# One weight pool kept open from the gate stage to branch A, and two staging buffers in place of three for the key and value stage

## The chip, the core and the metric

The kernel runs on one core of one Trainium2 chip. The core has five engines that run side by side, each through its own list of instructions in a fixed order: TensorE (PE in the profile) multiplies matrices, VectorE (DVE) and GpSimd (POOL) work on elements, ScalarE (ACT) applies functions and copies, and SyncE (SP) issues transfers. ACT issues transfers too, from the same list as its arithmetic, so a transfer or an operation that waits holds up everything behind it on ACT. All transfers run on 16 shared DMA engines. On-chip memory (SBUF) is given below as an address in KB of one partition; every tile takes all 128 partitions. PSUM has eight banks, and a bank can take the next product only when the last one has been read out of it.

The metric is the device time of one launch in microseconds, the median of several runs.

## The reference

One block of a transformer-like trunk over 1024 tokens of width 1024, all in float32:

```python
h = rmsnorm(x, ln1_g) * (1 + sc1) + sh1
q, k, v, cb, cc, cx, ga, gb = split(h @ w_in)          # eight column blocks of 1024
q, k = rmsnorm per head of q, k                        # 16 heads of 64
y_a = stick_breaking_attention(q, k, v)
y_b = cb * causal_dwconv(cc * cx, conv_w)
x = x + g1 * ((sigmoid(ga) * (y_a @ w_branch_a) + sigmoid(gb) * (y_b @ w_branch_b)) @ w_out)
h = rmsnorm(x, ln2_g) * (1 + sc2) + sh2
x = x + g2 * ((silu(h @ w_gate) * (h @ w_up)) @ w_down)
```

The six modulation vectors (sh1, sc1, g1, ...) come from a product of silu(c) with `ada_w`.

## The kernel before, in words

Every large product is done in three matmuls: each float32 operand is split into a high part (`hi`, written by ACT) and a rest (`lo`, written by DVE or POOL), and hi x hi, hi x lo and lo x hi are added up in PSUM. A weight therefore passes through a staging tile: SP loads it into `raw` (4 KB), ACT copies the high part out of `raw` into `whi`, DVE subtracts to make `wlo`, and then `raw` is free for the next load. How many `raw` tiles there are decides how far SP's loads run ahead of the splits.

The stages stand in this order:

1. **Start** (lines 141 to 330): load x transposed, compute the norm and the modulation, make `hh` and `hl` (the two parts of h, in four `big` tiles) one 128-row block k after the other, and begin the first product group, half of v, as the blocks come. Its weights come through `load_wq` and `split_wq`, from the pool `wpa` with three `raw` tiles and six tiles each of `whi` and `wlo`.
2. **Key and value stage** (lines 333 to 423): three column groups, `cc` = 0 (half of v), 1 and 2 (k), each over eight token tiles i. A tile's product takes 24 matmuls into one PSUM bank. In group 0 seven of the eight products are already in PSUM when this loop starts and only lack their last block, so seven `finish_v` follow each other closely. `finish_v` (line 391) copies the product out of PSUM with ACT (line 394), subtracts with DVE (line 395), which frees the bank, and stores the 4 KB tile `vs` to the DRAM scratch `d_v` from ACT's queue (line 396). `finish_k` (line 369) squares, normalizes and transposes a tile of k, makes its two parts in a tile `khl` (lines 385 and 386) and stores them to `d_k` with two transfers from ACT's queue (line 388). `vs` and `khl` share one tag with three buffers. A buffer can be written again when its store has landed. Beside this, `factors` (line 342) forms sums of h for the Strassen products, with POOL, ACT (line 358) and DVE, in the pool `phm` on the right side of SBUF.
3. **Gate stage** (lines 425 to 644): 20 rounds, each the product of h with two blocks of 128 columns, by Strassen's scheme with seven smaller products each (`half_prod`, lines 122 to 124). Weights come through `g_raw` and `g_split` (lines 428 and 435) from the pool `gw`, with two `raw` and four `whi` and `wlo` tiles of half the size. The first two products of the first two gates (`first_two`) stand ahead of the loop. For the loop, SP reloads parts of the factors: two transfers of 1 MB into `hh` and `hl` (line 581) and one of 2 MB into `ft6` (line 579). The loop begins with ACT's copy of the first product out of PSUM (line 617) and the split of the sums `ws` of the weights.
4. **Attention** (lines 653 to 887): the scores, scans and products of 16 heads, with the rest of v, the products of branch B and its projection mixed in as filler for PE. The filler's weights come through the same `g_raw` and `g_split`.
5. **Branch A's projection** (lines 908 to 939), again through `g_raw` and `g_split`; then the output projection (`w_o`), the second norm, the feed-forward products with pools of their own.

Each pool's place in SBUF is settled when it opens, on the left or the right end of what is free. `gw` is a pool named `wpg` at 167 to 191 KB during the gate stage. It opens at line 422, when `phm` has closed, on the place where `phm` was. It closes at line 645, and a pool `wpb` of the same size opens at 199 to 223 KB, where the tiles `ft5` and `ft4` were that the last gate's products read. `wpb` stays open until line 1005.

The order of each engine's instructions is settled at build time by a scheduler that knows the tiles' sizes and places and lets an instruction wait for the last user of the memory that it takes. A run of the program does not reorder anything.

Of the kernel before, what the change touches and what calls it, by code (L numbers as in the profile page):

```python
# [8 lines left out]
F32 = mybir.dt.float32  # L9
F32R = mybir.dt.float32r  # L10
# [6 lines left out]
P = 128  # L17
# [12 lines left out]
def block_kernel(tc, x, x_t, cols, ada_1, ada_2, ada_row, w_q, w_kv, w_v1, w_cg, w_a, w_b, w_o, w_g, w_u, w_d, out):  # L30
# [8 lines left out]
    def nm(s):  # L39
        uid[0] += 1  # L40
        return f"{s}_{uid[0]}"
# [1 line left out]
    def big():  # L43
        return bigp.tile([P, KT, 512], F32R, tag="big", bufs=4, name=nm("big"))

    wps = [None, 0, 0]

    def open_w(name, nraw, n):

        es = ExitStack()  # L50
        wps[:] = [es.enter_context(tc.tile_pool(name=name, bufs=1, reuse_waits="tile")), nraw, n]
        return es

    def load_w(src):

        wp, nraw, bufs = wps
        raw = wp.tile([P, 1024], F32, tag="raw", bufs=nraw, name=nm("raw"))
        nc.sync.dma_start(raw, src)
        hi = wp.tile([P, 1024], F32R, tag="whi", bufs=bufs, name=nm("whi"))
        lo = wp.tile([P, 1024], F32R, tag="wlo", bufs=bufs, name=nm("wlo"))  # L60
        nc.scalar.activation(hi, raw, AF.Copy)
        nc.vector.tensor_tensor(out=lo, in0=raw, in1=hi.bitcast(F32), op=ALU.subtract)
        return hi, lo
# [74 lines left out]

    md = ps_pj()

    sw = open_w("wpa", 3, 6)
    def in_order(i0):

        prev = {}
# [26 lines left out]
        ads.append(ad)  # L171

    def load_wq(qt):
        wp, nraw, bufs = wps
        raw = wp.tile([P, 1024], F32, tag="raw", bufs=nraw, name=nm("raw"))
        nc.sync.dma_start(raw, w_kv[0, qt])
        hi = wp.tile([P, 1024], F32R, tag="whi", bufs=bufs, name=nm("whi"))
        lo = wp.tile([P, 1024], F32R, tag="wlo", bufs=bufs, name=nm("wlo"))
        wraw.append(raw)
        wq.append((hi, lo))  # L180
# [153 lines left out]
    ap = s2.enter_context(tc.tile_pool(name="pha", bufs=1, reuse_waits="tile"))  # L334
# [34 lines left out]
    def finish_k(ps, i, ch):  # L369
        sq = ap.tile([P, 512], F32, tag="qsq", bufs=2, name=nm("qsq"))  # L370
        nc.scalar.activation(sq, ps, AF.Square)
        ss = ap.tile([P, 8], F32, tag="qss", bufs=3, name=nm("qss"))
        nc.vector.tensor_reduce(out=ss, in_=sq.rearrange("p (h d) -> p h d", d=DH), op=ALU.add, axis=AX.X)
        qn = ap.tile([P, 512], F32, tag="qn", bufs=2, name=nm("qn"))
        r = rstd_of(ss, 1.0 / DH, ap, 8)
        nc.vector.tensor_tensor(out=qn.rearrange("p (h d) -> p h d", d=DH),
                                in0=ps.rearrange("p (h d) -> p h d", d=DH),
                                in1=r.unsqueeze(2).broadcast_to([P, 8, DH]), op=ALU.mult)
        yield
        tr = ps_tr()  # L380
        for j in range(4):
            nc.tensor.transpose(tr[:, j * P:(j + 1) * P], qn[:, j * P:(j + 1) * P], ident)
        hl_ = ap.tile([P, 2, 512], F32R, tag="vs", bufs=3, name=nm("khl"))
        hi, lo = hl_[:, 0], hl_[:, 1]
        nc.scalar.activation(hi, tr, AF.Identity, scale=kgc)
        nc.vector.scalar_tensor_tensor(out=lo, in0=tr, scalar=kgc, in1=hi.bitcast(F32), op0=ALU.mult, op1=ALU.subtract)
        for e, t in ((0, hi), (1, lo)):
            nc.scalar.dma_start(d_k[e][4 * ch:4 * ch + 4, :, i * P:(i + 1) * P].rearrange("j p t -> p j t"),
                                t.rearrange("p (j t) -> p j t", j=4).bitcast(F32))

    def finish_v(ps, i, ch):
        vs = ap.tile([P, 8, P], F32R, tag="vs", bufs=3, name=nm("vs"))
        pv = ps.rearrange("p (h d) -> p h d", d=DH)
        nc.scalar.activation(vs[:, :, :DH], pv, AF.Copy)
        nc.vector.tensor_tensor(out=vs[:, :, DH:], in0=pv, in1=vs[:, :, :DH].bitcast(F32), op=ALU.subtract)
        nc.scalar.dma_start(d_v[8 * ch:8 * ch + 8, :, i, :].rearrange("h p d -> p h d"), vs.bitcast(F32))

    GR, NG, GS = 2, 2, 4
    tails = []
    for cc in range(3):  # L400
        w = wq if cc == 0 else [load_w(w_kv[cc, j]) for j in range(4)]
        for i in ((5, 6, 0, 1, 2, 3, 4, 7) if cc == 0 else range(8)):
            if cc == 0 and i < NPRE:
                ps = pss[i]
                mm_tok(ps, i, w, 7, 8)
            else:
                ps = ps_pj()
                mm_tok(ps, i, w, 0, 8)
            while len(tails) >= 2:
                next(tails.pop(0), None)  # L410
            if cc > 0:
                tails.append(finish_k(ps, i, cc - 1))
                next(tails[-1])
            else:
                finish_v(ps, i, 0)
            for _ in range(2 if cc else 0):
                next(ml, None)
            if (cc, i) == (2, 4):
                for _ in ml:
                    pass  # L420
                s2b.close()
                gws = ExitStack()
                gw = gws.enter_context(tc.tile_pool(name="wpg", bufs=1, side="right", reuse_waits="tile"))

    def g_bank():
        return ps_pj()
# [155 lines left out]
    for g, (sec, j) in enumerate(gates):  # L582
        raw, raw2 = raws
# [58 lines left out]
        for _ in range((0 if sec == 5 else 3) if g + 1 < len(gates) else 50):  # L642
            next(ml, None)
    sg_.close()
    gws.close()
    ftx.close()
    gws = ExitStack()
    gw = gws.enter_context(tc.tile_pool(name="wpb", bufs=1, side="right", reuse_waits="tile"))
    for e in range(2):
        nc.sync.dma_start((hh, hl)[e][1][:, :4].bitcast(F32), d_h[e])  # L650
    psA.close()
# [259 lines left out]
    for n in range(2):  # L911
        for k in range(KT):
            yr = fp.tile([P, 512], F32, tag="yr", bufs=2, name=nm("yr"))
            nc.sync.dma_start(yr, d_ya[n][:, k, :])
            tag, bufs = slots[n * KT + k]
# [23 lines left out]
            nc.vector.tensor_tensor(out=mlo[n][:, m, :], in0=sa, in1=mh[n][:, m, :].bitcast(F32), op=ALU.subtract)  # L939
    s3.close()  # L940
    fpool.close()
    psB.close()


# [2 lines left out]
    sw = ExitStack()  # L947
    wp = sw.enter_context(tc.tile_pool(name="wpd", bufs=1, reuse_waits="tile"))
# [49 lines left out]
    for ch in range(2):  # L998
        w = [] if ch else list(w_pre)
        for j in range(len(w) // 2, 4):  # L1000
            raw = load_raw(w_o[ch, j])
            w += [split(raw[:, c * 512:(c + 1) * 512]) for c in range(len(w) % 2, 2)]
        if ch == 1:
            swx.close()
            gws.close()
            rqs.close()
            s5 = ExitStack()
            hp = s5.enter_context(tc.tile_pool(name="phh", bufs=1, side="right", reuse_waits="tile"))

            h2t = {q: hp.tile([P, 4, 512], F32, name=f"h2b{q}") for q in ("01", "11", "t2", "00", "10")}  # L1010
            h2b = [[h2t[f"{e}{n}"] for n in range(2)] for e in range(2)]
            t2f = h2t["t2"]
        cs = slice(ch * 512, ch * 512 + 512)
        for i in range(8):
            n, t0 = i // 4, (i % 4) * P
            xi = dp.tile([P, 512], F32, tag="xr", bufs=3, name=nm("xr"))
            nc.scalar.dma_start(xi, x[i * P:(i + 1) * P, cs])
            ps = bank()
            for k in range(KT):
                nc.tensor.matmul(ps, mh[n][:, k, t0:t0 + P], w[k][0], start=(k == 0), stop=False)  # L1020
                nc.tensor.matmul(ps, mh[n][:, k, t0:t0 + P], w[k][1], start=False, stop=False)  # L1021
                nc.tensor.matmul(ps, mlo[n][:, k, t0:t0 + P], w[k][0], start=False, stop=(k == KT - 1))  # L1022
            tm = dp.tile([P, 512], F32, tag="tm", bufs=2, name=nm("tm"))
            nc.vector.tensor_tensor(out=tm, in0=ps, in1=g1b[:, cs], op=ALU.mult)
            if ch == 0:
                nc.vector.tensor_tensor(out=tm, in0=tm, in1=xi, op=ALU.add)
                nc.scalar.dma_start(d_x1[i, :, cs], tm)
                continue
            x1 = dp.tile([P, D], F32, tag="x1", bufs=2, name=nm("x1"))
            nc.scalar.dma_start(x1[:, :512], d_x1[i, :, :512])  # L1030
            nc.vector.tensor_tensor(out=x1[:, cs], in0=tm, in1=xi, op=ALU.add)
            nc.scalar.dma_start(d_x1[i, :, cs], x1[:, cs])
            ss = dp.tile([P, 1], F32, tag="ss", bufs=3, name=nm("ss"))
            xn = dp.tile([P, D], F32, tag="xn", bufs=2, name=nm("xn"))
            nc.scalar.activation(xn, x1, AF.Square, accum_out=ss)  # L1035
            r = rstd_of(ss, 1.0 / D, dp, 1)
            nc.scalar.activation(xn, x1, AF.Copy, scale=r[:, 0:1])
            if tails:
                norm2_tail(*tails.pop())
            tails.append((i, xn))  # L1040
            if i == 4:
                bh, bl = big(), big()
            if i == 5:
                for e in range(2):
                    split_big(bh[:, 4 * e:4 * e + 4], bl[:, 4 * e:4 * e + 4], h2b[e][0])
# [11 lines left out]
    for key, src in (((0, 0), w_g), ((0, 1), w_u), ((1, 0), w_g)):  # L1057
        raw = load_raw(src[key[0]])
# [291 lines left out]
```

## Time and profile before

| | |
|---|---|
| runs, us | 1946.02, 1945.4, 1941.25; median 1945.4 |
| profiled execution, us | 1945.62, of which the span from first to last instruction 1943.8 |
| PE busy in the span | 1853.6 us (95%) |
| DVE, ACT, POOL busy | 1462.3, 864.6, 673.7 us |
| mean DMA rate | 179 GB/s |
| mean granted TensorE clock | 0.986 |

The profile is one execution. A row of its timeline has the start and the duration in us, the engine (with a q where it is the issue of a transfer), the line, the operation, what it writes and reads, how many equal ones were merged into the row, and in brackets how long the engine had been idle and what ended that. A row of the waits has who waited for whom, the sum in us, how many times, and the longest. Lines named in rows are those of the listing above. Names stand without their numbers, so that all `vs` tiles are `vs`, and the matrix-product banks of the early stages are `pj`.

### The profile page before, as it was taken

How to read it: one execution, taken by the hardware profiler on the slowest of the kernel's cores; microseconds unless marked ns; L12 is line 12 of the kernel's file. 1: busy time of each engine (PE TensorE's matmuls, PEld its weight loads, DVE VectorE, ACT ScalarE, POOL GpSimd, SP SyncE). 2: the span in 40 equal slices, each digit the busy share in tenths (PEclk: the TensorE clock that was granted, in tenths of full speed). 3: DMA queues.
4: the chain of work that ended last, by engine and by line, in shares of the span. 5: the costliest groups of instructions: out<-in, count | busy, mean ns of one | idle time of the engine just before them, and what ended most of it. 6: DMA issues, size and time to landing. Idle time of an engine off the chain costs nothing.

```text
span 1943.8 us, 25154 instructions
## 1 busy us (share of the span) xinstructions
PE 1853.6 (95%) x8869; PEld 1519.5 (78%) x8869; DVE 1462.3 (75%) x1927; ACT 864.6 (44%) x1597; POOL 673.7 (35%) x475
## 2 busy tenths in 40 slices
PE   7899999998999999998999999979999999999899
PEld 4678767777888888887888788867888888878587
DVE  8865687778664799998999644499988788743854
ACT  4442343223333677776777421464444434422221
POOL 3694547978231001111000000065454444301713
PEclk8899999999999999999999999999999999999999
DMA  6465544334445756559554535323343334399566
GB/s 276 162 208 172 190 154 160 136 114 152 170 171 197 214 158 189 169 167 302 161 161 128 189 130 193 133 82 136 146 173 152 141 143 171 119 347 321 218 221 224
DMA packets 151149, 347.47 MB, mean 179 GB/s; under 512 B 15088, under 2 KB 52208, under 8 KB 149104
## 3 DMA queue, kind: packets, MB, share of 16 engines
q1 hardware_dynamic: 74000, 218.80, 34.4%
q10 hardware_dynamic: 76016, 123.40, 17.6%
q0 software_dynamic: 1008, 3.67, 0.5%
q8 instruction: 70, 1.15, 0.2%
q14 instruction: 55, 0.45, 0.1%
HBM read 235.19 MB, written 110.62 MB: 178 GB/s over the span
## 4 chain that ended last, share of the span: by engine, by line
PE 43%; DVE 10%; issue 3%; DMA 3%; ACT 2%; POOL 1%; ACTq 0%; SPq 0%; DVEq 0%; POOLq 0%
PE e L122 6%; PE e L124 6%; PE e L123 6%; PE e L1203 3%; PE e L1204 3%; PE e L1202 3%; PE pj L785 3%; PE pj L786 3%; PE pj L787 3%; DVE pt L710 2%; DVE wlo L965 2%; PE e L1020 1%; PE e L1022 1%; PE e L1021 1%; PE tr L726 1%
## 5 line engine op out<-in xcount | busy, mean ns | idle before, releaser
L710 DVE TENSOR_TENSOR_SCAN pt<-pt,dm 128x256 f32<-128x256 f32 (+7 forms) x128 | 173.9, 1363 | 5.3 <-ACT pt L705 5.1
L123 PE MATMUL e<-big,whi 128*128 128x512 f32 x352 | 138.0, 392 | 7.8 <-DVE big L127 7.8
L122 PE MATMUL e<-big,whi 128*128 128x512 f32 x352 | 137.7, 392 | 0.8 <-ACT c L1118 0.8
L124 PE MATMUL e<-big,wlo 128*128 128x512 f32 x352 | 137.5, 391 | 0.0
L1203 PE MATMUL e<-wlo,f 128*128 128x512 f32 (+1 forms) x319 | 123.1, 386 | 9.5 <-DVE wlo L965 9.5
L124 PE MATMUL pj<-big,wlo 128*128 128x512 f32 x320 | 127.0, 398 | 5.1 <-DVE wlo L127 5.1
L113 POOL TENSOR_SCALAR rs_m<-ss 128x1 f32<-128x1 f32 x8 | 2.0, 245 | 365.3 <-ACT xn L1035 365.3
L122 PE MATMUL pj<-big,whi 128*128 128x512 f32 x320 | 128.0, 400 | 0.4 <-ACT whi L438 0.4
L276 PE MATMUL pj<-whi,big 128*128 128x512 f32 x352 | 116.3, 410 | 11.6 <-ACT big L263 8.9
L123 PE MATMUL pj<-big,whi 128*128 128x512 f32 x320 | 127.1, 397 | 0.0
L705 ACT ACTIVATE pt<-z,rq 128x512 f32<-128x512 f32 (+2 forms) x192 | 112.3, 587 | 30.5 <-PE z L704 17.6
L1204 PE MATMUL e<-whi,f 128*128 128x512 f32 (+1 forms) x319 | 121.8, 382 | 0.0
L1202 PE MATMUL e<-whi,f 128*128 128x512 f32 (+1 forms) x319 | 118.5, 383 | 2.0 <-ACT fs L1142 1.4
L127 DVE TENSOR_TENSOR c<-e,c 128x512 f32<-128x512 f32 x154 | 102.8, 681 | 21.1 <-PE e L124 21.1
L829 POOL TENSOR_TENSOR ybl<-cy,ybh 128x512 fp32r<-128x512 f32 x16 | 29.0, 1810 | 255.7 <-ACT ybh L828 242.9
L438 ACT ACTIVATE whi<-raw 128x512 fp32r<-128x512 f32 x116 | 72.7, 633 | 94.4 <-PE pj L123 32.6
L706 ACT ACTIVATE sg<-z,rq 128x512 f32<-128x512 f32 (+1 forms) x192 | 112.7, 590 | 1.3 <-DVE mb L851 1.3
L127 DVE TENSOR_TENSOR c<-pj,c 128x512 f32<-128x512 f32 x140 | 93.2, 681 | 24.3 <-PE pj L124 24.1
L127 DVE TENSOR_TENSOR wlo<-ws,whi 128x512 fp32r<-128x512 f32 x80 | 73.6, 939 | 50.0 <-ACT whi L438 49.8
L730 DVE TENSOR_TENSOR atl<-tr,ath 128x512 fp32r<-128x512 f32 (+1 forms) x192 | 100.3, 544 | 10.7 <-ACT ath L729 10.3
L127 POOL TENSOR_TENSOR ws<-raw,raw 128x512 f32<-128x512 f32 x41 | 57.9, 1412 | 144.1 <-DMA raw<-w_cg 80.7
L729 ACT ACTIVATE ath<-tr 128x512 fp32r<-128x512 f32 (+1 forms) x192 | 90.4, 498 | 37.8 <-PE tr L726 12.7
(250 smaller groups left out, 5641.9 us busy)
## 6 DMA issues: line engine op xcount, KB each, us to landing
f<-d_f SPq DMA_DIRECT2D x77, 512.0 KB, 4.4
d_f<-fs ACTq DMA_DIRECT2D x70, 512.0 KB, 2.6
raw<-w_cg SPq DMA_DIRECT2D x40, 512.0 KB, 3.4
mada<-ada ACTq DMA_DIRECT2D x32, 512.0 KB, 4.2
raw<-w_g SPq DMA_DIRECT2D x24, 512.0 KB, 3.2
raw<-w_u SPq DMA_DIRECT2D x23, 512.0 KB, 3.2
d_k<-khl ACTq DMA_DIRECT2D x32, 256.0 KB, 2.2
d_q<-gt ACTq DMA_DIRECT2D x32, 256.0 KB, 2.1
```

Of the source, the lines that this page charges most:

```text
L122: nc.tensor.matmul(ps, wh[:, k, :], fh[:, k, :], start=(k == 0), stop=False)
L123: nc.tensor.matmul(ps, wh[:, k, :], fl[:, k, :], start=False, stop=False)
L124: nc.tensor.matmul(ps, wl[:, k, :], fh[:, k, :], start=False, stop=(k == 3))
L127: eng.tensor_tensor(out=out, in0=a, in1=b, op=op)
L276: nc.tensor.matmul(ps, a, b, start=(k == 0 and q == 0), stop=(k == KT - 1 and q == 2))
L705: nc.scalar.activation(pt[:, off + s0:off + s0 + m], z[:, :m], AF.Sigmoid, scale=rq[:, 1, i, h:h + 1])
L706: nc.scalar.activation(sg[:, s0:s0 + m], z[:, :m], AF.Sigmoid, scale=rq[:, 0, i, h:h + 1])
L710: nc.vector.tensor_tensor_scan(out=pt[:, rev], data0=pt[:, rev], data1=dm[:, rev], initial=0.0, op0=ALU.mult, op1=ALU.add)
L730: nc.vector.tensor_tensor(out=tl[:, :nb, c0:c0 + P], in0=src, in1=th[:, :nb, c0:c0 + P].bitcast(F32), op=ALU.subtract)
L1202: nc.tensor.matmul(o, sh, w[0][:, c], start=(j == 0), stop=False)
L1203: nc.tensor.matmul(o, sh, w[1][:, c], start=False, stop=False)
L1204: nc.tensor.matmul(o, sl, w[0][:, c], start=False, stop=(j == NJ - 1))
```

## The change

One pool `gw`, named `wpl`, with two `raw` tiles and four half-size `whi` and `wlo` tiles, opens ahead of the first weight pool at 85 to 109 KB and closes after branch A's projection. It takes the place of `wpg` and `wpb`. The start stage and the key and value stage no longer have `raw` tiles of their own: they use the two of this pool. `vs` and `khl` have two buffers in place of three. `wpa` now holds only `whi` and `wlo` and lies at 109 to 157 KB; the pools behind it on the left move up by 12 KB (start, key and value stage) or 24 KB (gate stage, attention), and the attention's pools on the right move into the 24 KB that `wpb` had. The first weights of the output projection (`wpx`) move with them by 24 KB; everything behind that lies where it was. No arithmetic and no transfer is added or removed.

```diff
-    wps = [None, 0, 0]
+    wps = [None, 0]
-    def open_w(name, nraw, n):
+    def open_w(name, n):
         es = ExitStack()
-        wps[:] = [es.enter_context(tc.tile_pool(name=name, bufs=1, reuse_waits="tile")), nraw, n]
+        wps[:] = [es.enter_context(tc.tile_pool(name=name, bufs=1, reuse_waits="tile")), n]
         return es
     def load_w(src):
-        wp, nraw, bufs = wps
-        raw = wp.tile([P, 1024], F32, tag="raw", bufs=nraw, name=nm("raw"))
+        wp, bufs = wps
+        raw = gw.tile([P, 1024], F32, tag="raw", bufs=GR, name=nm("raw"))
         nc.sync.dma_start(raw, src)
...
-    sw = open_w("wpa", 3, 6)
+    GR, NG, GS = 2, 2, 4
+    gws = ExitStack()
+    gw = gws.enter_context(tc.tile_pool(name="wpl", bufs=1, reuse_waits="tile"))
+    sw = open_w("wpa", 6)
...
     def load_wq(qt):
-        wp, nraw, bufs = wps
-        raw = wp.tile([P, 1024], F32, tag="raw", bufs=nraw, name=nm("raw"))
+        wp, bufs = wps
+        raw = gw.tile([P, 1024], F32, tag="raw", bufs=GR, name=nm("raw"))
...
-        hl_ = ap.tile([P, 2, 512], F32R, tag="vs", bufs=3, name=nm("khl"))
+        hl_ = ap.tile([P, 2, 512], F32R, tag="vs", bufs=2, name=nm("khl"))
...
-        vs = ap.tile([P, 8, P], F32R, tag="vs", bufs=3, name=nm("vs"))
+        vs = ap.tile([P, 8, P], F32R, tag="vs", bufs=2, name=nm("vs"))
...
-    GR, NG, GS = 2, 2, 4
     tails = []
...
                 s2b.close()
-                gws = ExitStack()
-                gw = gws.enter_context(tc.tile_pool(name="wpg", bufs=1, side="right", reuse_waits="tile"))
...
     sg_.close()
-    gws.close()
     ftx.close()
-    gws = ExitStack()
-    gw = gws.enter_context(tc.tile_pool(name="wpb", bufs=1, side="right", reuse_waits="tile"))
...
     fpool.close()
+    gws.close()
     psB.close()
...
             swx.close()
-            gws.close()
             rqs.close()
```

## The prediction

> **What bounds the kernel now.** I read the page's head, then the busy time by stage, then what PE waited for.
>
> ```profile
> span 1943.8 us, 25154 instructions
> PE 1853.6 (95%) x8869; PEld 1519.5 (78%) x8869; DVE 1462.3 (75%) x1927; ACT 864.6 (44%) x1597; POOL 673.7 (35%) x475
> ```
>
> ```profile
> 85.00:192.00 107.00, 104.91 (x485) 85.74 (x484) 64.17 (x77) 38.43 (x62) 77.21 (x63) 1.00 0.57 180
> 192.00:620.00 428.00, 413.51 (x1768) 325.26 (x1767) 307.96 (x370) 144.74 (x240) 247.05 (x162) 0.99 0.45 158
> 620.00:1085.00 465.00, 441.64 (x2727) 384.90 (x2726) 426.85 (x612) 338.07 (x726) 29.14 (x20) 0.99 0.63 186
> 1085.00:1132.00 47.00, 47.00 (x199) 37.84 (x199) 24.65 (x38) 14.48 (x24) 0.00 (x0) 0.97 0.57 188
> 1132.00:1300.00 168.00, 163.98 (x742) 133.13 (x741) 90.51 (x135) 63.98 (x106) 21.76 (x25) 1.00 0.41 141
> ```
>
> The columns are the stretch, its length, then busy time of PE, PEld, DVE, ACT and POOL, the granted clock, DMA share and GB/s. The stretches are key and value stage, gates, attention, branch A, output projection with second norm. PE is the bound in every one of them: it idles 2.1 of 107 us in the key and value stage and nothing in branch A. So a change of buffers can win only what PE waits at the places it touches, and loses whatever new wait reaches PE. The built order of the changed program has the same instructions on every engine (8811 PE rows of the listing, 1934 ACT, 587 SP), so nothing is priced by count, only by waits and order.
>
> **What can be won.** The moved weight tiles touch three borders. Key and value to gates:
>
> ```profile
> 206.86 0.57 PE L122 MATMUL pj<-ft,whi 128*128 128x512 f32 x1 [2.06 <-ACT whi L438]
> ```
>
> Gates to attention (PE's waits between 596 and 660):
>
> ```profile
> PE z L703 <- ACT sg L706: 1.7, 1, 1.7
> PE pj L805 <- DVE wlo L127: 0.5, 1, 0.5
> PE pj L804 <- DVE vs L810: 0.4, 1, 0.4
> ```
>
> Branch A to output projection: PE is full to 1132 and loses 4 us in the next 168, spread over the second norm, so nothing is left there. At the second border the filler's weights no longer wait for the last gate products that read `ft5` and `ft4`, and stand two places earlier in SP's queue. I count the two small waits, 0.5 + 0.4 = 0.9 us, as gone (term C, -0.9; bounds 0 and all three, -2.6; the 1.7 hangs on a sigmoid and not on a weight, so I leave it). The 2.06 at the first border is no wait for the pool that moves, as term B shows.
>
> **Term A: two buffers for `vs`, and the burst of seven.** ACT, DVE and PE around 92 to 102:
>
> ```profile
> 92.94 0.60 ACT L394 ACTIVATE vs<-pj 128x512 fp32r<-128x512 f32 x1
> 94.69 1.07 ACT L61 ACTIVATE whi<-raw 128x1024 fp32r<-128x1024 f32 x1 [0.30 <-PE pj L276]
> 97.14 1.04 ACT L61 ACTIVATE whi<-raw 128x1024 fp32r<-128x1024 f32 x1
> 98.09 0.58 ACT L394 ACTIVATE vs<-pj 128x512 fp32r<-128x512 f32 x1
> ```
>
> ```profile
> 93.81 0.68 DVE L395 TENSOR_TENSOR vs<-pj,vs 128x512 fp32r<-128x512 f32 x1
> 99.12 2.31 DVE L62 TENSOR_TENSOR wlo<-raw,whi 128x1024 fp32r<-128x1024 f32 x1
> 101.36 0.68 DVE L395 TENSOR_TENSOR vs<-pj,vs 128x512 fp32r<-128x512 f32 x1
> ```
>
> ```profile
> 102.19 0.47 PE L276 MATMUL pj<-whi,big 128*128 128x512 f32 x1 [0.74 <-DVE vs L395]
> 96.00:101.45 5.45, 5.45 (x25) 4.17 (x23) 1.00 1.01 329
> L396 ACTq DMA_DIRECT2D d_v<-vs x3: 384/422/1803, 93.3 to 94.7; - x3
> DMA to landing us min/median/max: 4.1/5.2/5.8
> ```
>
> The first two `vs` of the burst come from the transpose banks; the third, at 92.94, frees on DVE at 93.81 + 0.68 = 94.49 the bank of the first product of k, the fourth (101.36, done at 102.04) that of the second. PE runs k's first product from 96.00 to 101.45 (24 matmuls; the window counts one that overlaps its edge) and then waits 0.74 for the second bank. With two buffers the third `vs` waits until the first store has landed: issued at 93.3, plus 4.1, is 97.4. In the changed order ACT's copy stands behind both weight splits (94.69, 97.14), and DVE's subtraction behind the second L62, which ends at 101.4. So the third takes the fourth's place, 98.09 on ACT and 101.36 on DVE, and k's first product starts at 102.19 in place of 96.00. Its 5.45 us are then moved whole behind the wait: the second starts at 107.64, not 102.19, +5.45. Its own bank comes at about 104 and costs nothing more; later ones, some 5.5 us apart with landings of 4 to 6, come before PE needs them. Queued behind the waiting ACT copy stand `factors`' copies and k's squares (L371), for which PE has its other banks.
>
> Something comes back ahead of it. DVE's L62 at 75.26 now stands behind the modulation's last sums:
>
> ```profile
> 75.26 1.21 DVE L62 TENSOR_TENSOR wlo<-raw,whi 128x1024 fp32r<-128x1024 f32 x1
> 79.37 0.80 PE L214 MATMUL pj<-ones,acc 128*128 128x1 f32 x3 [0.48 <-DVE acc L204]
> ```
>
> That lets PE's 0.48 go: term A is +5.0. Lower bound: DVE takes the subtraction as soon as ACT's copy ends (98.67), done 99.35, PE from 99.5: 99.5 + 5.45 - 102.19 - 0.48 = +2.3. Upper bound +5.45. I keep the row's own order on DVE, so 5.0.
>
> **Term B: two buffers for `khl`, and the reload of the factors.** The end of the stage on ACT and SP:
>
> ```profile
> 198.81 0.69 ACT L385 ACTIVATE khl<-tr,cst 128x512 fp32r<-128x512 f32 x1 [5.29 <-PE tr L382]
> 199.53 1.15 ACTq L388 DMA_DIRECT2D d_k<-khl  x2
> 201.11 0.69 ACT L385 ACTIVATE khl<-tr,cst 128x512 fp32r<-128x512 f32 x1 [1.61 <-PE tr L382]
> 201.83 3.33 ACTq L388 DMA_DIRECT2D d_k<-khl  x2
> 205.21 1.08 ACT L617 ACTIVATE c<-pj 128x512 f32<-128x512 f32 x2 [3.41 <-issue]
> 206.18 2.19 ACT L438 ACTIVATE whi<-ws 128x512 fp32r<-128x512 f32 x4
> 189.44 0.81 SPq L581 DMA_DIRECT2D big<-d_t  x2
> 194.73 0.32 SPq L579 DMA_DIRECT2D ft<-d_t  x1
> ```
>
> The stores of the sixth k tile, and those of the tiles before it, by line 388 between 193 and 195 and between 163 and 190:
>
> ```profile
> L388 ACTq DMA_DIRECT2D d_k<-khl x2: 366/366/366, 193.6 to 194.4; - x2
> DMA to landing us min/median/max: 11.4/12.0/12.7
> ...
> L388 ACTq DMA_DIRECT2D d_k<-khl x10: 366/366/369, 163.9 to 188.4; - x10
> DMA to landing us min/median/max: 2.2/2.2/3.8
> ```
>
> Stores that land in 2.2 us take 11.4 and 12.7 beside the 4 MB that SP reloads: 193.6 + 11.4 = 204.9 and 194.4 + 12.7 = 207.1. The last `khl`, at 201.11, takes the third buffer now; with two it takes that tile's and waits until 207.1, +6.0 on ACT. Behind it on ACT stand its two stores, the copies of line 617 and the split L438 that PE waits for at 206.86. Before, the two stores took 3.33 to issue with four others under way; at 207.1 two have landed, so 0.37 each as in the ten above, the second after L386: L617 follows some 2 us after `khl` and not 4.1. That gives 6.0 - 2.1 = +3.9, all on PE, which already waits. Bounds: only the earlier landing counts, 204.9, giving 3.8 - 2.1 = +1.7; the slow issue stays, +6.0. I take 3.9, since ten issues of twelve took 0.37.
>
> [...]
>
> **Term D: two `raw` tiles for three, 0.** Each load now waits for one more split.
>
> ```profile
> 63.42 34.43 SPq L58 DMA_DIRECT2D raw<-w_kv  x7
> L58 SPq DMA_DIRECT2D raw<-w_kv x8: 327/328/328, 47.7 to 97.5; - x8
> DMA to landing us min/median/max: 3.1/3.3/4.4
> 142.19 18.15 SPq L430 DMA_DIRECT2D raw<-w_q  x4
> ```
>
> The loads go one release later, and the start's last one too, but their splits come 6 us or more behind the landing or wait for PE anyway, and the first gates' weights, loaded from 142, are used at 192. What covers this is PE's product of 5.45 us in progress and its spare banks. Without that cover one landing (3.3 to 4.4) stands on ACT ahead of work that frees a bank; that is a rival.
>
> **Sum.** 5.0 + 3.9 - 0.9 + 0 = +8.0. Bounds 2.3 + 1.7 - 2.6 = +1.4 and 5.45 + 6.0 = +11.4. The profiled execution took 1945.62 (span 1943.8 and 1.8 around it), so 1953.6; the median of the three runs is 0.2 lower, so **1953.4**, within 1946.8 and 1956.8.
>
> **The rivals.** [...]
>
> *Faster* (R2): the stores land in 2.2 us also in the burst, the third `vs` finds its buffer by 96 and DVE free, and the gates' first split comes early, because its weights have a place of their own. Then the waits of 0.48, 2.06, 0.5, 0.4 and 1.7 go: 1945.4 - 5.1 = 1940.3. It decides where landings fall under some 3 us. Against: 4.1 is the least in the burst, and the 2.06 hangs on ACT's `khl` chain.
>
> *Also the staging tiles cost* (R3): a load's landing of 3.3 to 4.4 on ACT, with its split of 1.07 behind it, reaches a PSUM bank once in the k tiles: 1953.4 + 5 = 1958.4. For: both first gates' splits now stand among k's tiles on ACT. Against: PE's 2.1 us of idle time in 107.
>
> That the change doesn't do what it says is out: places and order are settled at build time, and the waits for a store two tiles back are in them.
>
> **How the numbers follow.** Forecast 0.70, R1 0.07, R2 0.08, R3 0.15. A measurement of this kernel tells 0.3% (5.8 us) from no change, so the borders are 1939.6 and 1951.2. Slower: R3 and all of the forecast but 0.06 at its lower bound, 0.79. Same: that 0.06, R1, and 0.03 of R2: 0.16. Faster: 0.05 of R2. The range starts at the lower bound, 1947, and ends at 1961, R3 with a landing at its longest and term B at its upper bound; R2 and a little at each end are left out.
>
> **What would show it.** After: at the end of the v group PE waits some 6 us for L395 ahead of k's first product, and no longer 0.74 ahead of the second; the last L385 of the k stage is released by a `d_k` landing; PE's wait for L438 ahead of the first `ft` product grows from 2.06 to about 6; the two waits at 805 and 804 are gone; from the attention on every stage has its old length. It is wrong if `d_k` lands fast at that place, if DVE takes the third `vs` ahead of L62, or if a stage that only moved in SBUF changes its length.

## The result, and the profile after

| | before | after |
|---|---|---|
| median of the runs, us | 1945.4 (7 runs, 1941.25 to 1949.39) | 1949.12 (7 runs, 1947.88 to 1951.71) |
| after / before | | 1.0025, 95% interval 1.0014 to 1.0036 |
| profiled execution, us | 1945.62 (span 1943.8) | 1949.12 (span 1947.2) |
| mean granted TensorE clock | 0.986 | 0.981 |

The change costs 3.7 us by the medians and 4.9 (2.7 to 7.0) by the ratio. The forecast was 8.0 more. The head of the page of after:

```profile
span 1947.2 us, 25170 instructions
PE 1849.1 (95%) x8869; PEld 1524.6 (78%) x8869; DVE 1462.6 (75%) x1927; ACT 866.3 (44%) x1597; POOL 671.6 (34%) x475
```

PE has as many matmuls as before and is busy 4.5 us *less* (1853.6 before), though its clock was lower. So two things happened: PE waits longer, and its matmuls got shorter. First the waits. The timeline of after around the end of the v group (start, duration, engine, line, what it writes and reads, idle time before it and its releaser):

```profile
94.50 1.04 ACT L61 ACTIVATE whi<-raw 128x1024 fp32r<-128x1024 f32 x1
95.45 0.58 ACT L397 ACTIVATE vs<-pj 128x512 fp32r<-128x512 f32 x1
...
98.15 2.28 DVE L62 TENSOR_TENSOR wlo<-raw,whi 128x1024 fp32r<-128x1024 f32 x1
100.35 0.68 DVE L398 TENSOR_TENSOR vs<-pj,vs 128x512 fp32r<-128x512 f32 x1
...
101.17 0.77 PE L279 MATMUL pj<-whi,big 128*128 128x512 f32 x1 [9.06 <-DVE vs L398]
```

The copy into the third `vs` (line 397, 394 before) stands behind both splits on ACT, its subtraction (398) behind the second one on DVE, and PE starts k's first product at 101.17. The store of the first `vs`, whose buffer it takes, had landed by then: issued at 89.4, 5.2 us to landing, 94.6. So it is the order on DVE that sets the end of the wait. PE came to that point at 92.11 and waited 9.06; before it waited 0.74, ahead of the second product. Behind the wait PE's granted clock was low in after (stretch, its length, PE's busy time and matmuls, granted clock, DMA share, GB/s), where in before it was 1.00 from 92 to 116:

```profile
100.00:104.00 4.00, 2.83 (x7) 0.50 0.54 153
104.00:108.00 4.00, 4.00 (x15) 0.74 1.12 368
```

So k's first product took 7.8 us (its first matmul started at 101.17, that of the second product at 109.00) and not the 5.45 of before, and k's third product started 6.7 us late. Part of that was taken up again: between 130 and 158 PE idled 1.4 us in before and not at all in after. What is left at the end of k's tiles is seen in the last tile but one, before and after:

```profile
198.17 0.60 PE L382 MATMUL tr<-dm,qn 128*128 128x128 f32 x4
```

```profile
202.96 0.60 PE L385 MATMUL tr<-dm,qn 128*128 128x128 f32 x4
```

+4.8. Next the end of the stage, on ACT and PE, and the stores of the `khl` that is two tiles older (with the landing times):

```profile
198.43 1.17 ACTq L391 DMA_DIRECT2D d_k<-khl  x2
203.59 0.69 ACT L388 ACTIVATE khl<-tr,cst 128x512 fp32r<-128x512 f32 x1 [5.19 <-PE tr L385]
212.41 0.69 ACT L388 ACTIVATE khl<-tr,cst 128x512 fp32r<-128x512 f32 x1 [8.13 <-DMA d_k<-khl]
215.29 2.19 ACT L438 ACTIVATE whi<-ws 128x512 fp32r<-128x512 f32 x4
...
215.97 0.79 PE L122 MATMUL pj<-ft,whi 128*128 128x512 f32 x1 [6.45 <-ACT whi L438]
```

```profile
L391 ACTq DMA_DIRECT2D d_k<-khl x2: 366/366/366, 198.4 to 199.2; - x2
DMA to landing us min/median/max: 6.4/9.8/13.1
```

The last `khl` is released by a landing of `d_k`: 199.2 + 13.1 = 212.3. PE starts the first `ft` product at 215.97, not 206.86: +9.1 in all, so +4.3 from this wait beside the +4.8.

From there the program runs 10 us behind, and gets less late on the way. The same instruction of the gate stage at its beginning and end, before and after:

```profile
232.94 0.33 ACTq L536 DMA_DIRECT2D d_q<-gt  x1
...
601.83 0.33 ACTq L600 DMA_DIRECT2D d_sga<-c  x1
```

```profile
243.30 0.33 ACTq L536 DMA_DIRECT2D d_q<-gt  x1
...
610.96 0.33 ACTq L600 DMA_DIRECT2D d_sga<-c  x1
```

+10.4 at the beginning, +9.1 at the end. And all matmuls of one line of branch A's projection on `ya`, before and after (count, shortest/median/longest ns of one, first to last start):

```profile
L785 PE MATMUL pj<-ya,whi x128: 393/395/397, 1093.6 to 1182.5; 128*128 128x512 f32 x128
```

```profile
L782 PE MATMUL pj<-ya,whi x128: 389/389/389, 1099.7 to 1186.0; 128*128 128x512 f32 x128
```

PE is full there in both (busy in all of these 88.9 and 86.3 us, at a granted clock of 1.00), and the stage takes 88.9 us before and 86.3 after. (By these rows branch A ends at 1182.5 in before; the row of the prediction that goes from 1085 to 1132 holds only its first half.) The shift is +6.1 where it begins and +3.5 where it ends, and +3.4 at the end of the span. The 1.3 us between +9.1 and +10.4 behind the second wait are clock. PE and its granted clock from there on, before and after:

```profile
206.00:210.00 4.00, 3.14 (x8) 0.65 0.61 186
210.00:214.00 4.00, 4.00 (x17) 0.93 0.00 0
```

```profile
216.00:220.00 4.00, 4.00 (x10) 0.50 0.00 0
220.00:224.00 4.00, 4.00 (x15) 0.73 0.00 0
```

The columns are as above. The first 8 us ran at a mean of 0.62 after and 0.79 before, which is 1.4 us of PE.

**The border between gates and attention** gave nothing. The two small waits for L805 and L804 are gone, and the one ahead of the first scores grew from 1.7 to 2.8 (waits of PE from 600 to 665 in after):

```profile
PE z L700 <- ACT sg L703: 2.8, 1, 2.8
```

**The matmuls.** The groups of the gate stage in the view by line (count | busy us, mean ns of one | idle before), before and after:

```profile
L122 PE MATMUL pj<-big,whi 128*128 128x512 f32 x320 | 128.0, 400 | 0.4 <-ACT whi L438 0.4
L122 PE MATMUL pj<-ft,whi 128*128 128x512 f32 x240 | 96.4, 402 | 5.4 <-ACT whi L438 5.4
```

```profile
L122 PE MATMUL pj<-big,whi 128*128 128x512 f32 x320 | 125.9, 394 | 0.7 <-ACT whi L438 0.7
L122 PE MATMUL pj<-ft,whi 128*128 128x512 f32 x240 | 97.6, 407 | 10.3 <-ACT whi L438 10.3
```

With `big` as moving data a matmul is 6 ns shorter, with `ft` 5 ns longer. I laid each matmul's row beside its instruction in the built program, which has the addresses of both operands, and took the time from its start to the next one's, for all neighbours of 512 columns between 204 and 640 us (mean ns; "begin" is the address in bytes past a multiple of 128):

| moving data | before: weights begin at 96 | after: weights begin at 0 |
|---|---|---|
| `big`, begins at 0 | 233.3 (868 pairs) | 227.2 (874) |
| `ft6`, at 0 | 233.4 (231) | 228.9 (232) |
| `ft4`, at 96 | 227.4 (234) | 233.2 (234) |
| `ft5`, at 96 | 229.3 (216) | 233.4 (204) |

Where both begin alike PE starts a matmul every 227 to 229 ns, where they don't every 233. The weights and `ft` tiles on the right side of SBUF begin at 96 past a multiple of 128, the weights and moving data on the left at 0, and the change took the weights from the right side to the left. Of the neighbours in the two traces those that differ by 32 or 96 fall from 2327 to 516: 1811 x 6.2 ns = 11.2 us of PE, part of it where PE waits anyway. The prediction had no such term.

### The profile page after: what moved, and what is told of

It is laid out like the page before. It is cut to its first block, busy times and chain, and to the rows that moved or that the text cites. A ratio compares the mean times of both kernels' runs of the same rounds, so it can differ in the third digit from the quotient of the medians.

```text
span 1947.2 us, 25170 instructions
## 1 busy us (share of the span) xinstructions
PE 1849.1 (95%) x8869; PEld 1524.6 (78%) x8869; DVE 1462.6 (75%) x1927; ACT 866.3 (44%) x1597; POOL 671.6 (34%) x475
## 4 chain that ended last, share of the span: by engine, by line
PE 52%; DVE 16%; POOL 6%; issue 5%; DMA 5%; ACT 3%; ACTq 0%; SPq 0%; DVEq 0%; POOLq 0%
PE e L123 6%; PE e L124 6%; PE e L122 6%; DVE pt L707 4%; PE e L1200 3%; PE e L1201 3%; PE e L1199 3%; PE pj L124 3%; PE pj L122 3%; PE pj L123 3%; PE pj L782 2%; PE pj L783 2%; PE pj L784 2%; DVE atl L727 2%; DVE sg L709 2%
## 5 line engine op out<-in xcount | busy, mean ns | idle before, releaser
L122 PE MATMUL pj<-big,whi 128*128 128x512 f32 x320 | 125.9, 394 | 0.7 <-ACT whi L438 0.7
L123 PE MATMUL pj<-big,whi 128*128 128x512 f32 x320 | 124.9, 390 | 0.0
L122 PE MATMUL pj<-ft,whi 128*128 128x512 f32 x240 | 97.6, 407 | 10.3 <-ACT whi L438 10.3
```

The source lines that it names most:

```text
L122: nc.tensor.matmul(ps, wh[:, k, :], fh[:, k, :], start=(k == 0), stop=False)
L123: nc.tensor.matmul(ps, wh[:, k, :], fl[:, k, :], start=False, stop=False)
```

## The experiments

The time of the kernel before in the comparisons below was 1943.9 to 1945.1; ratios are to it.

| kernel | median, us | ratio (95% interval) |
|---|---|---|
| the change | 1949.1 | 1.0025 (1.0014 to 1.0036) |
| before, two buffers only | 1953.6 | 1.0045 (1.0028 to 1.0062) |
| change, third buffer for `vs` and the last `khl` | 1938.0 | 0.9966 (0.9952 to 0.9980) |
| change, third buffer for `vs` | 1945.0; 1942.4 | 1.0002 (0.9988 to 1.0017); 0.9999 (0.9985 to 1.0012) |
| change, spare tile for the last `khl` | 1942.0 | 0.9999 (0.9986 to 1.0012) |
| before, right side 32 bytes lower | 1941.0 | 0.9985 (0.9973 to 0.9998) |
| change, its weights 32 bytes higher | 1954.3 | 1.0047 (1.0035 to 1.0059) |
| change, attention's weights on the right again | 1951.1 | 1.0035 (1.0021 to 1.0049) |
| change, both third buffers and right side 32 bytes lower | 1938.4 | 0.9967 (0.9955 to 0.9979) |

**Both kernels profiled once more**, with no edit, to see what belongs to one execution.

> The kernel before, unchanged, profiled once more. Theory 1 (the differences of the two traces behind 900 us belong to single executions): at least one of the three things that the first trace had and the changed kernel's trace had not is gone: PE's wait of 4.40 us for ath at 916 with half the clock behind it, matmuls 233 ns apart in place of 227 between 200 and 1200 us, PE's clock of 0.66 at 920. Theory 2 (they belong to where the tiles lie): all three are there again, within 1 us and 1 ns. Span 1941 to 1946.

> The changed kernel, unchanged, profiled once more. Both theories: the waits of PE at 92 (9.06) and 209 (6.45) are there within 1 us, since they are in the program's waits. Theory 1: the wait for ath at 928 (1.68) or the distance of the matmuls in branch A (227 ns) differs from the first trace. Theory 2: both repeat. Span 1946 to 1950.

Measured 1940.47 and 1948.27. In before PE's wait around 918 us was 1.45, no longer 4.40, and the clock stayed full; the wait and the clock in the first and the second execution:

```profile
920.79 0.58 PE L741 MATMUL o<-ath,vt 128*128 128x256 f32 x1 [4.40 <-ACT ath L729]
```

```profile
922.00:926.00 4.00, 4.00 (x21) 0.50 0.86 323
926.00:930.00 4.00, 4.00 (x21) 0.83 0.48 155
```

```profile
919.83 0.39 PE L741 MATMUL o<-ath,vt 128*128 128x256 f32 x1 [1.45 <-ACT ath L729]
```

```profile
922.00:926.00 4.00, 4.00 (x28) 1.00 1.02 395
```

But the distance of the matmuls came again. Branch A's line on `ya` in the second executions of before and of after:

```profile
L785 PE MATMUL pj<-ya,whi x128: 393/395/397, 1090.1 to 1179.0; 128*128 128x512 f32 x128
```

```profile
L782 PE MATMUL pj<-ya,whi x128: 389/389/389, 1099.3 to 1185.7; 128*128 128x512 f32 x128
```

88.9 and 86.4, as in the first executions within 0.1 us. The waits at the changed buffers, which both theories expected within 1 us, did not repeat so closely: PE waited 6.17 and 4.64 us in after where it had waited 9.06 and 6.45.

```profile
101.15 0.77 PE L279 MATMUL pj<-whi,big 128*128 128x512 f32 x1 [6.17 <-DVE vs L398]
```

Its start was the same, 101.15 and 101.17; PE had come there 2.9 us later. At the end of k's tiles the second pair shows +4.8 like the first, at the first `ft` product +7.9 (214.77 against 206.86), so +3.1 from the second wait.

So each theory holds for a part. Some 5 us that the first pair of traces shows as won around 920 belong to one execution: in the second pair the shift is +9.2 where branch A begins (1090.1 against 1099.3) and +6.7 where it ends. What branch A wins belongs to the program.

**Two buffers alone.** In before:

```diff
-        hl_ = ap.tile([P, 2, 512], F32R, tag="vs", bufs=3, name=nm("khl"))
+        hl_ = ap.tile([P, 2, 512], F32R, tag="vs", bufs=2, name=nm("khl"))
-        vs = ap.tile([P, 8, P], F32R, tag="vs", bufs=3, name=nm("vs"))
+        vs = ap.tile([P, 8, P], F32R, tag="vs", bufs=2, name=nm("vs"))
```

> The kernel before, with two buffers in place of three for the tiles vs and khl and nothing else: the same pools at the same places otherwise. If the two waits are the change's whole cost and what came back is a matter of executions (theory 1): PE's waits at 92 and 209 as in the changed kernel (some 9 and 6.5 us), and the whole 4 to 9 us over before, 1949 to 1954, not told from the changed kernel by more than 2 us. If what came back (5.2 around 916 to 945, 3.1 in branch A and the output projection) belongs to the moved weight tiles (theory 2): it stays away, 9 over before, 1953 to 1955. If the two buffers aren't the cause: 1945.

1953.6, ratio 1.0045: 8.8 us (5.4 to 12.1). Both waits stand in its timeline:

```profile
102.35 0.77 PE L276 MATMUL pj<-whi,big 128*128 128x512 f32 x1 [5.44 <-DVE vs L395]
...
216.33 0.79 PE L122 MATMUL pj<-ft,whi 128*128 128x512 f32 x1 [5.56 <-ACT whi L438]
```

The waits are shorter than the 9 and 6.5 us of the expectation; the first product of k starts at nearly the same place (102.35) as in the change. The two buffers cost more alone (8.8) than the change that contains them (4.9), so the rest of the change gains some 4 us, though the intervals of the two overlap; branch A keeps 88.9 here (1102.4 to 1191.3). This is what the second theory expected, and the first gave a range wide enough to hold it too.

**Third buffers again.** In the change, `phm` (named `mp` in the code) has two 4 KB tiles `ts` that are free while v is finished and after `factors` has ended. Every third `vs` and the last `khl` go there, and `phm` closes with the stage:

```diff
+        vn[0] += 1
+        vs = (mp.tile([P, 8, P], F32R, tag="ts", bufs=2, name=nm("vs")) if vn[0] % 3 == 0 else
+              ap.tile([P, 8, P], F32R, tag="vs", bufs=2, name=nm("vs")))
...
+        hl_ = (mp.tile([P, 2, 512], F32R, tag="ts", bufs=2, name=nm("khl")) if (ch, i) == (1, 7) else
+               ap.tile([P, 2, 512], F32R, tag="vs", bufs=2, name=nm("khl")))
...
-                s2b.close()
...
+    s2b.close()
     s2.close()
```

> The changed kernel with a third buffer again where it waits: every third vs, and the last khl, lies in a tile of the factors' pool that is free at that time. If the two waits are the cost (4.4 to 5.0 and 3.9 us): both are gone and it takes 8 to 9 us less than the changed kernel, 1940 to 1942, 3 to 5 under before. If only the first matters: 1944 to 1945. If the cost lies elsewhere (staging tiles, places): 1948 to 1950.

1938.0, 2 us under its range, ratio 0.9966. PE doesn't wait for `vs` at the v group's end any more, and the end of the stage reads:

```profile
200.34 0.69 ACT L389 ACTIVATE khl<-tr,cst 128x512 fp32r<-128x512 f32 x1 [1.61 <-PE tr L385]
...
207.44 0.50 PE L122 MATMUL pj<-ft,whi 128*128 128x512 f32 x1 [3.46 <-ACT whi L442]
```

This is 0.6% under the change and beats both kernels. It still has two `raw` tiles where before has three, and no cost of that is to be seen.

Then each tile alone, the first half and the second half of that edit. First `vs`, measured twice:

> The changed kernel with a third buffer for vs alone (in the factors' pool), and two for khl. If the two waits add up as predicted (5.0 and 3.9): PE's wait ahead of k's first product is gone, the one ahead of the first ft product stays at 4 to 7 us, and it takes 1941 to 1945, 4 to 7 over the kernel with both spare tiles' 1938 less than 5. If the second wait hides behind the first: 1938.

> The kernel with the spare tile for vs alone once more, since its 10 runs lay 14 us apart: 1942 to 1945, 4 to 7 under the changed kernel and 4 to 7 over the kernel with both spare tiles (1938).

1945.0 and 1942.4; the second time the landing of `d_k` releases the last `khl` still:

```profile
205.16 0.69 ACT L388 ACTIVATE khl<-tr,cst 128x512 fp32r<-128x512 f32 x1 [6.14 <-DMA d_k<-khl]
...
208.73 0.79 PE L122 MATMUL pj<-ft,whi 128*128 128x512 f32 x1 [4.46 <-ACT whi L442]
```

Then the last `khl` alone:

> The changed kernel with a spare tile for the last khl alone (in the factors' pool), two buffers for vs as in the change. If the two waits add up: the one ahead of the first ft product comes down to 2 to 3.5 us, the one ahead of k's first product stays at 6 to 9, and it takes 1943 to 1946, 3 to 7 under the changed kernel. If the second wait hides behind the first: 1949, no change.

1942.0, 1 us under the range; its PE keeps the first wait (7.35, start at 101.08) and of the second keeps 0.36, less than the 2 to 3.5 expected:

```profile
209.42 0.50 PE L122 MATMUL pj<-ft,whi 128*128 128x512 f32 x1 [0.36 <-ACT whi L438]
```

By the ratios each alone gives back 0.23 to 0.26% (some 5 us), both 0.59% (11.5 us). So the two waits add up and neither hides behind the other; the 1.5 us beyond two times 5 are within the intervals.

**Where the tiles begin.** In before, 32 bytes at the right end, so that the whole right side lies 32 bytes lower and its weights begin at 64 past a multiple of 128:

```diff
     rqp = rqs.enter_context(tc.tile_pool(name="rqp", bufs=1, side="right", reuse_waits="tile"))
+    rqp.tile([P, 8], F32, name="pad")
```

> The kernel before with 32 bytes more in the rightmost pool, so that everything on the right side begins 32 bytes lower; nothing else. Before, the tiles on the right begin at 32 past a multiple of 64 bytes, those on the left at 0. Theory (places): matmuls follow 227 ns apart when moving tile and weights begin alike in this sense, and 233 when they differ; in the first trace 2327 neighbouring matmuls differ (14.4 us in all), in the changed kernel's 516. Then all of them come to 227 here, and with the share that the changed kernel kept of its 11.2 us (4 to 5), some 5 to 7 us come off: 1938 to 1941. Rival (the 24 KB move itself, or the pool that stays open, gained it): distances stay 233 and 1945.

1941.0, ratio 0.9985: 2.9 us off (0.4 to 5.3), less than expected. The built program has all matmuls in the order of before, so only addresses differ. Branch A's line:

```profile
L786 PE MATMUL pj<-ya,whi x128: 392/392/394, 1091.8 to 1179.0; 128*128 128x512 f32 x128
```

87.2 us: between the 88.9 and the 86.4. In the gates `big` came to 229.1 ns, not 227. 64 bytes apart was better here than 32 or 96, and not as good as alike.

The other way round, in the change 32 bytes ahead of the weights of the open pool and 32 behind, so that nothing else on the left moves off its multiple of 64:

```diff
     gw = gws.enter_context(tc.tile_pool(name="wpl", bufs=1, reuse_waits="tile"))
+    gw.tile([P, 8], F32, name="pad")
+    gws.enter_context(tc.tile_pool(name="wpm", bufs=1, reuse_waits="tile")).tile([P, 8], F32, name="pad2")
```

> The changed kernel with 32 bytes ahead of the weight tiles in the open pool and 32 more behind it: only the weights from the gates to branch A begin at 32 past a multiple of 64, all else on the left at 0 as before. Theory (places): big, ft6 and ya against whi and wlo at 233 ns, ft5 and ft4 at 227, as in the kernel before; 4 to 5 us come on: 1953 to 1955, like the kernel before with two buffers. Rival: 1948 to 1950.

1954.3, ratio 1.0047, 0.22% over the change: 4.3 us, or 1 to 7 by the two intervals together. That is level with the two buffers alone. The order of the matmuls is that of the change. Branch A:

```profile
L784 PE MATMUL pj<-ya,whi x128: 393/396/397, 1099.6 to 1188.5; 128*128 128x512 f32 x128
```

88.9 again. 64 bytes, in a pool that stays open at the same place, take away about as much as the change had won. One point went otherwise: `ft4` begins at 96 and the weights at 32 there, and the distance was 233.3, not 227. Alike in the last 64 bytes isn't enough.

With the third buffers and the right side 32 bytes lower:

> The changed kernel with a third buffer where it waited, as in the experiment with the spare tiles, and the 32 bytes in the rightmost pool. Theory (places): the last 516 unlike pairs (ft5 and ft4 in the gates, the output projection's first weights) come to 227, 3.2 us on PE, of which 1 to 3 reach the end: 1935 to 1937. Rival: 1938, no change.

1938.4, ratio 0.9967: no change against 0.9966. The expectation's premise fell: `ft4` and `ft5` begin at 64 here and the weights at 0, and the distance stayed at 233.2 ns (231 and 212 pairs), so little was there to win.

The second half of the change undone: the pool closes behind the gates, and the attention's and branch A's weights lie on the right again.

```diff
     ftx.close()
+    gws.close()
+    gws = ExitStack()
+    gw = gws.enter_context(tc.tile_pool(name="wpb", bufs=1, side="right", reuse_waits="tile"))
```

> The changed kernel, but the open pool is closed behind the gates, and the attention's and branch A's weights lie in a pool of their own on the right again, at 199 KB, as before. Theory (places): from the attention to branch A weights begin at 32 past a multiple of 64 against big and ya at 0, 233 ns there as before (some 1100 pairs), 227 with big in the gates; 2 to 4 us over the changed kernel, 1950 to 1953, most of it between 1090 and 1140 us and in the attention's stretches where PE is full. Term C of the prediction (the border between gates and attention) would add 0.9. Rival (the gain lies in the start and the gates): 1948 to 1950.

1951.1, ratio 1.0035; the intervals of this and of the change overlap, so the time alone decides nothing. The trace does: branch A takes 88.9 us again, while the gates keep their 227 with `big`.

```profile
L785 PE MATMUL pj<-ya,whi x128: 393/395/397, 1099.9 to 1188.8; 128*128 128x512 f32 x128
```

**The distance by itself.** Groups of 64 matmuls on two tiles that begin at multiples of 128; each group takes slices that begin a few bytes later:

```diff
+    for n in range(N):
+        o = 8 + n % 2 * 128
+        nc.tensor.matmul(banks[0], ws[:, o:o + 128], mv[:, 0:0 + 512], start=(n == 0), stop=(n == N - 1))
```

> None of the block is computed: 16 groups of 64 matmuls (128 by 128 weights, 512 columns, the kernel's own form) run back to back from two tiles that are written once, with nothing else on any engine; the groups differ only in how many bytes past a multiple of 128 the moving data and the weights begin. Theory (places alone): 227 ns from one matmul to the next where both begin alike (0 and 0, 32 and 32, 64 and 64), 233 where they differ by 32 or 96, between them (229) at 64. Rival (the distance needs DMA or other engines' traffic beside it, or a certain part of SBUF): 227 in all groups.

Six of the groups, by line (shortest/median/longest ns of one, first to last start): moving data and weights at 0 and 0, 0 and 32, 32 and 0, 32 and 32, 64 and 32, 64 and 64.

```profile
L49 PE MATMUL ps<-mv,ws x64: 389/389/397, 22.2 to 36.4; 128*128 128x512 f32 x64
L52 PE MATMUL ps<-mv,ws x64: 392/395/397, 36.7 to 51.4; 128*128 128x512 f32 x64
...
L61 PE MATMUL ps<-mv,ws x64: 393/395/398, 81.5 to 96.2; 128*128 128x512 f32 x64
L64 PE MATMUL ps<-mv,ws x64: 389/389/397, 96.4 to 110.7; 128*128 128x512 f32 x64
...
L73 PE MATMUL ps<-mv,ws x64: 392/395/397, 140.8 to 155.5; 128*128 128x512 f32 x64
...
L79 PE MATMUL ps<-mv,ws x64: 388/389/398, 170.4 to 184.7; 128*128 128x512 f32 x64
```

From the 63 distances between starts of each group (mean ns):

| moving, weights (bytes past a multiple of 128) | ns |
|---|---|
| 0, 0; 32, 32; 64, 64 | 226.7; 226.7; 227.0 |
| 0, 32; 0, 96; 32, 0; 32, 64; 64, 32 | 233.3; 234.1; 233.3; 233.3; 233.3 |
| 64, 0; 96, 32 | 228.9; 229.1 |
| 0, 64; 32, 96 | 233.4; 233.4 |
| 0, 16; 16, 16 | 226.7; 230.0 |
| 0, 128 (weights a whole 128 further) | 232.4 |

From 20 to 220 us the DMA share was at most 0.01 and DVE, ACT and POOL did nothing, and the 233 is there beside the 227, so the rival falls. Both tiles alike gives 227 in three groups of four, 32 or 96 apart gives 233 in five of five. The rule in the expectation isn't the whole of it: 64 apart gave 229 or 233, here and in the kernels with the lowered right side, and a whole 128 apart gave 232, in the one group that ran beside the transfers of the output (DMA share 0.57 from 230 to 240 us), so whether the address or the transfers cost those 6 ns isn't shown.

## Why the prediction was right or wrong

The direction was right, and the time lies inside the range, 4.3 us under the forecast. That it comes so near is in part luck: the sum lacked a loss by the clock behind both waits (2.4 and 1.4 us) and a gain of about 4 us by the new addresses, which go opposite ways. By its own steps:

- **Term A, 5.0.** The mechanism is confirmed: the order on ACT and DVE is the one forecast, `vs` behind both splits, PE starts k's first product when DVE's subtraction is done (101.17 and 101.15 in the two executions), and the wait of 0.48 at line 214 is gone. The size, +4.8 at the end of k's tiles in both pairs, agrees partly by luck. DVE was done 1.0 us earlier than forecast (PE at 101.17, not 102.19), the low clock behind the wait added 2.4 us to k's first product, and some 1.9 of the 6.7 us were taken up later in the stage; none of the three is in the sum. That PE waited 9.06, not some 6, belongs to one execution, in which it came to the place 3.9 us earlier than before; in the other it waited 6.17. A start that is faster is lost in a wait whose end DVE sets.
- **Term B, 3.9.** Confirmed: the stores landed in 6.4 and 13.1 us beside the reload, the last `khl` waited for the second of them, and PE lost 4.3, in the second pair 3.1. The 1.4 us at a lower clock behind the longer wait were not in the sum.
- **Term C, -0.9.** The two waits went as said, and 1.1 us came up at the wait that I left out. Mis-sized: 0.
- **Term D, 0.** Right: with both third buffers and two `raw` tiles the kernel is 0.34% faster than before, so no cost of the staging tiles shows (some 4 us of the 6.6 gained are the addresses), and R3 falls. R1, the sum without term B, falls with the landings of 6.4 and 13.1 us that the last `khl` waited for. R2 falls with the landings too: those in after that released a `khl` or a `vs` in the two bursts took 3.6 us or more.
- **What failed** is the sentence "nothing is priced by count, only by waits and order", and with it the sign that "from the attention on every stage has its old length". Branch A went from 88.9 to 86.4 us in every pair of traces, the gates won 1.2, with the same matmuls in the same order. The prediction named a stage that changes its length by a mere move in SBUF as what would make it wrong, and gave it no price, no rival and no place in the bounds.
- **The sum in place of it:** two buffers +8.8 (measured alone; forecast 5.0 + 3.9), the weights' new place -4.3 (what the 64 bytes took away). That leaves +4.5, against the +4.9 measured by the ratio. Each of these figures has an interval of 2 to 3.4 us to either side, so that they agree to 0.4 says little. The traces bear out the gain more closely: 1.2 in the gates and 2.6 in branch A in the first pair, 1.6 and 2.5 in the second. The total is about half of the forecast because a gain half as large stood in no sentence of it.

The first trace alone would have misled: it shows 5 us won around 920 us that the second execution of before doesn't confirm.

## What to carry to other kernels

Price a move in SBUF too: where PE is full, compare where the moving data and the weights begin, since 32 bytes between them cost 6.6 ns on a matmul of 512 columns here (233.3 against 226.7), and a pad of one small tile won 2.9 us in one kernel and cost 4.3 in the other. A double buffer in place of a triple one was paid here where tiles came in a burst (+4.8 us) and where their store landed beside a reload (+4.3); spare tiles that were idle at those places gave back both waits. And profile the unchanged kernel twice before explaining a difference of a few microseconds in one stage.

## What the runs showed of the hardware

- Matmuls of 512 float32 columns followed each other 226.7 ns apart in the groups where moving data and weights both begin at 0 or both at 32 past a multiple of 128 bytes, and 233.3 to 234.1 where they begin 32 or 96 bytes apart; in two kernels and their variants it is 227 to 229 and 233. So what one operand cost here depended on where the other lay. Where that arises, and why 64 bytes apart gave 228.9 and 229.1 ns in two groups and 233.4 in two others, wasn't found.
- A wait of PE was paid twice here: behind 4.40 us the granted clock was 0.50 from 922 to 926 us and 0.83 in the next 4, behind 1.45 us at the same place it stayed at 1.00 from 918 to 930. A shorter wait was no safeguard: behind the 2.06 us ahead of the first `ft` product in before, the clock was 0.65 from 206 to 210, and behind 1.50 us at that place in the second execution it was 1.00 from 206 to 216.
- Stores of 256 KB that land in 2.2 us (median of ten between 163 and 190 us in before, where all transfers together ran at 118 GB/s) took 6.4 and 13.1 us in after beside 4 MB of loads from another queue (335 GB/s from 198 to 213 us), though the two were issued 0.8 us apart.
